# Decoder block on one core: the first norm's token scale summed from the feature-major input

## The chip, the cores and the metric

The kernel runs on one core of one Trainium2 chip. The metric is the device time of one execution in microseconds (us); less is better. A core has five engines with instruction streams of their own: PE (TensorE, matrix products; its weight loads are shown as PEld), DVE (VectorE), ACT (ScalarE), POOL (GpSimd) and SP (SyncE, which here only issues transfers). Engines wait for each other through semaphores, and each engine takes its instructions strictly in order.

## What is computed

One decoder block on 512 tokens of width 1024: a gated feed-forward (width 2816), a mixer, and a second feed-forward, each with a norm before and after it. The change concerns the start of the first feed-forward:

```
def rms_norm(x, g):
    xf = x.astype(jnp.float32)
    y = xf * lax.rsqrt(jnp.mean(xf * xf, axis=-1, keepdims=True) + NORM_EPS)
    return (y * g.astype(jnp.float32)).astype(x.dtype)

def swiglu(x, w_gu, w_down):
    g, u = jnp.split(x @ w_gu, 2, axis=-1)
    return (jax.nn.silu(g) * u) @ w_down
...
    f = swiglu(rms_norm(h, ffn1_pre_g[l]), ffn1_w_gu[l], ffn1_w_down[l])
    h = h + MACARON_SCALE * rms_norm(f, ffn1_post_g[l])
```

The norm's scale, one over the root of the mean square, is one number for each token. It can therefore be multiplied into the product with `w_gu` afterwards, as long as it is there before the gate's nonlinearity.

## The kernel before

Activations lie feature-major in the first feed-forward: features on the 128 partitions (eight chunks of 128, index `k`), the 512 tokens along the free axis. Every fp32 product is made of three matmuls on parts: a value is split into a rounded high part and the rest (a copy on ACT, a subtraction on DVE), and high times high, high times low and low times high are added up in PSUM.

Stages of the first feed-forward, in the order in which PE runs them:

1. `first_unscaled`: four output chunks (`f1f` banks) accumulate over `k = 0..7`, twelve 128x512 matmuls for each `k`, from `xk` (a 128x512 piece of `xt`, the feature-major input, in the tiles `xs`) times the norm's gain, and from `wk` (tiles `wf`). ACT makes `u1h` and the high weights, DVE makes `u1l` and the low weights. The scale is not yet applied. This loop lies in a block in which the written order holds (`tc.manual_schedule()`); elsewhere a scheduler sets each engine's order by a simulated timeline.
2. The `f1g` chunks: eight more output chunks of 24 matmuls 128x512 each, with weights that `wload` fetches (`wraw`) and `wsplit` splits into high and low (tiles `w`: line 104 on ACT, line 105 on DVE).
3. The `f1X`, `f1Y`, `f1Q` products of `paired`: the other columns in a scheme of seven block products of 128x256 matmuls, on sums of weight blocks (`f1L`, `f1R`, `f1M`, `f1N`, splits `f1W`) and of activation blocks (`u1m`).

`token_scale` makes the scale. It has the input a second time, token-major, as `xin` (four loads of 128x1024, tiles `x`): ACT squares each with a sum along the row, DVE adds the epsilon, POOL raises to the power -1/2, DVE puts the 128 values on a diagonal (`n1d`), which is split (`n1dd`) and multiplied by a matrix of ones. The product, bank `rb`, holds each token's scale on every partition, and ACT copies it to `rbc`. Its `yield 2` places these matmuls two chunks later on PE. Only then come `tail`, which multiplies the banks by `rbc` (`f1gs`, `f1us`), takes the tanh on ACT (`f1s`) and forms the gated product `f1p`, and `scaled`, which multiplies `xs` in place by gain and `rbc` (line 707) and forms the `u1m` splits.

Pools that matter: `big` (19 buffers), `t4p` (8 buffers of 128x1024: `wraw`, `x`, `f1L`, `f1R`, `u1ts`), `t2p` (10 buffers of 128x512) and eight PSUM banks. All these loads are issued by SP in one queue.

Of the kernel before, what the change touches and what calls it, by code (L numbers as in the profile page):

```python
# [8 lines left out]
F32 = mybir.dt.float32  # L9
F32R = mybir.dt.float32r  # L10
AF = mybir.ActivationFunctionType
ALU = mybir.AluOpType
# [4 lines left out]
P = 128  # L17
# [11 lines left out]
NT = T // P  # L29
D = 1024  # L30
KD = D // P
FF = 2816
KF = FF // P
EPS = 1e-6
# [8 lines left out]
def hybrid_block_kernel(ctx, tc, x, xt, g1, w_first, gains, gu1, gs1, dn1, ds1, w_x, w_gate, w_q, w_k, w_v, w_gl, w_ga, w_pl, w_pa,  # L43
                        w_o, gu2, gs2, dn2, ds2, vecs, bd, sinks, rope, mask, out):
    nc = tc.nc
    V, A, G, PE, SP = nc.vector, nc.scalar, nc.gpsimd, nc.tensor, nc.sync

    const = ctx.enter_context(tc.tile_pool(name="const", bufs=1))
# [7 lines left out]
    def bank(name):  # L56
        return psum.tile([P, 512], F32, name=name, tag="bank")

    def t4(name, dtype=F32):
        return t4p.tile([P, 1024], dtype, name=name, tag="t4")  # L60

    def t2(name, dtype=F32):
        return t2p.tile([P, 512], dtype, name=name, tag="t2")

    def b8(name, shape, dtype=F32):
        return big.tile(shape, dtype, name=name, tag="b8")

    def sm(name, n=1):
        return small.tile([P, n], F32, name=name, tag=f"sm{n}")
# [15 lines left out]
    RAHEAD = 3  # L85
# [7 lines left out]
    def wload(upto):  # L93
        while len(raws) < min(upto, wcap[0]):
            n = len(raws)
            raw = t4(f"wraw{n}")
            wdma.append(SP.dma_start(raw, worder[n]))
            raws.append(raw)

    def wsplit(upto):  # L100
        while len(wready) < min(upto, wcap[0]):
            n = len(wready)
            w = b8(f"w{n}", [P, 2, 1024], F32R)
            A.copy(w[:, 0, :], raws[n])  # L104
            V.tensor_tensor(out=w[:, 1, :], in0=raws[n], in1=w[:, 0, :].bitcast(F32),  # L105
                            op=ALU.subtract)
            wready.append((w[:, 0, :], w[:, 1, :]))
            wload(n + 1 + RAHEAD)
# [9 lines left out]
    def start(gen):  # L118
        n = next(gen, None)
        if n is not None:  # L120
            live.append([gen, n])
# [22 lines left out]
    xv = x.rearrange("(t p) d -> t p d", p=P)  # L144
# [7 lines left out]
    for k in range(KD):  # L152
        xk, wk = xs[k // 4][:, k % 4, :], wf[k // 4][:, k % 4, :]
        SP.dma_start(xk, xt[k])
        SP.dma_start(wk, w_first[k])
        first_in.append((xk, wk))
    xin = []
    for t in range(NT):
        wload(min(t + 1, RAHEAD))
        xin.append(t4(f"x_{t}"))  # L160
        SP.dma_start(xin[t], xv[t])
    ident = const.tile([P, P], F32, name="ident")
    make_identity(nc, ident)
    ones = t2("ones", F32R)[:, :P]
    G.memset(ones.bitcast(F32), 1.0)
    mhalf = const.tile([P, 1], F32, name="mhalf")
    G.memset(mhalf, -0.5)

    def rstd(ms, name):
        r = sm(name)  # L170
        G.tensor_tensor(out=r, in0=ms, in1=mhalf, op=ALU.pow)
        return r
# [4 lines left out]
    def at(u, part, k, tok):  # L177
        return u[part][k // 4][:, k % 4, tok]
# [466 lines left out]
    def moving(raw, name, mv):  # L645
        lo_, hi_ = slice(0, 256), slice(256, 512)
        t = [t4(f"{name}ts{i}").rearrange("p (k t) -> p k t", k=4) for i in range(2)]
        a, b = raw

        def split(i, z, sign=1.0):  # L650
            o = b8(f"{name}m{i}", [P, 2, 4, 256], F32R)
            mv[i] = o[:, 0], o[:, 1]
            A.activation(o[:, 0], z, AF.Copy, scale=sign)
            V.scalar_tensor_tensor(out=o[:, 1], in0=z, scalar=sign, in1=o[:, 0].bitcast(F32), op0=ALU.mult,
                                   op1=ALU.subtract)

        V.tensor_tensor(out=t[0], in0=a[:, :, lo_], in1=a[:, :, hi_], op=ALU.subtract)
        V.tensor_tensor(out=t[1], in0=b[:, :, hi_], in1=t[0], op=ALU.add)
        split(6, t[1], -1.0)
        split(5, t[0])  # L660
        yield 1
        V.tensor_tensor(out=t[0], in0=b[:, :, hi_], in1=a[:, :, hi_], op=ALU.subtract)
        split(7, t[0])
        yield 1
        V.tensor_tensor(out=t[1], in0=t[1], in1=b[:, :, lo_], op=ALU.subtract)
        split(4, t[1])
# [8 lines left out]

    rbc = t2("rbc")

    def token_scale(after):
        dhs = []
        for t in range(NT):  # L680
            ms = sm(f"n1ms{t}")
            A.activation(xin[t], xin[t], AF.Square, scale=1.0 / 32.0, accum_out=ms)
            me = sm(f"n1me{t}")
            V.tensor_scalar_add(me, ms, EPS)
            r = rstd(me, f"n1r{t}")
            d = t2(f"n1d{t}")[:, :P]
            V.tensor_scalar_mul(d, ident, r)
            dh = t2(f"n1dd{t}", F32R)[:, :2 * P].rearrange("p (s t) -> p s t", s=2)
            A.copy(dh[:, 0, :], d)
            V.tensor_tensor(out=dh[:, 1, :], in0=d, in1=dh[:, 0, :].bitcast(F32), op=ALU.subtract)  # L690
            dhs.append(dh)
        yield 2
        b = bank("rb")
        for t, dh in enumerate(dhs):
            for i in range(2):
                PE.matmul(b[:, t * P:(t + 1) * P], lhsT=ones, rhs=dh[:, i, :], start=i == 0, stop=i == 1)
        A.copy(rbc, b)
        after()
        start(scaled())

    mv1 = {}

    def scaled():
        lo_, hi_ = slice(0, 256), slice(256, 512)
        for k in range(KD):
            xk = first_in[k][0]
            V.scalar_tensor_tensor(out=xk, in0=xk, scalar=g1v[:, k:k + 1], in1=rbc, op0=ALU.mult, op1=ALU.mult)
            if k % 4 == 3:
                yield 1
        for i, half, tok in ((1, 0, lo_), (2, 1, lo_), (3, 1, hi_)):  # L710
            o, z = b8(f"u1m{i}", [P, 2, 4, 256], F32R), xs[half][:, :, tok]
            mv1[i] = o[:, 0], o[:, 1]
            A.copy(o[:, 0], z)
            V.tensor_tensor(out=o[:, 1], in0=z, in1=o[:, 0].bitcast(F32), op=ALU.subtract)
            if i == 2:
                yield 1
        yield from moving(xs, "u1", mv1)

    def first_unscaled(u, name, done):
        bs = [bank(f"{name}{i}") for i in range(4)]  # L720
        with tc.manual_schedule():
            for k in range(KD):
                xk, wk = first_in[k]
                if k % 2 == 0:
                    w = b8(f"{name}w{k}", [P, 2, 2, 512], F32R)
                wh, wl = w[:, k % 2, 0, :], w[:, k % 2, 1, :]
                uh, ul = at(u, 0, k, ALL), at(u, 1, k, ALL)
                A.activation(uh, xk, AF.Copy, scale=g1v[:, k:k + 1])
                A.copy(wh, wk)
                V.scalar_tensor_tensor(out=ul, in0=xk, scalar=g1v[:, k:k + 1], in1=uh.bitcast(F32),  # L730
                                       op0=ALU.mult, op1=ALU.subtract)
                V.tensor_tensor(out=wl, in0=wk, in1=wh.bitcast(F32), op=ALU.subtract)
                for lw, rx, n in ((wh, uh, 0), (wh, ul, 1), (wl, uh, 2)):
                    for i in range(4):
                        PE.matmul(bs[i], lhsT=lw[:, i * P:(i + 1) * P], rhs=rx, start=k == 0 and n == 0,
                                  stop=k == KD - 1 and n == 2)
        wsplit(2)
        start(token_scale(lambda: [done(i, b) for i, b in enumerate(bs)]))

    chunk1, blocked1 = gate_up(u1, "f1", first_unscaled, lambda: (gs1, mv1), lambda: rbc, ds1)  # L740
    g_post, g_pre = gain_pair(1, 2, "g_b1")
    u2 = new_u("u2")
# [17 lines left out]
    z = const.tile([P, KD], F32, name="z")  # L760
# [18 lines left out]
    for i in range(2):  # L779
        raw = t4(f"bdraw{i}")  # L780
        A.dma_start(raw, bd[i])
        t = b8(f"bd{i}", [P, 2, D], F32R)
# [193 lines left out]
    def sig_gate(c, src, name):  # L976
        w = wget()
        b = bank(f"{name}g{c}")
        feat_chunk(b, w, u2, ALL)
        s = t2(f"{name}s{c}")  # L980
        A.activation(s, b, AF.Tanh, scale=0.5)
        tick()
        wh, wl = wget()
        b = bank(f"{name}p{c}")
        for k in range(KD):
            ks = slice(k * P, (k + 1) * P)
            sh, sl = src[k // 4]
            mm3(b, wh[:, ks], wl[:, ks], sh[:, k % 4, :], sl[:, k % 4, :], k == 0, k == KD - 1)
        tick()
        return s, b  # L990
# [36 lines left out]
    for c in range(KD):  # L1027
        s, b = sig_gate(c, yl, "gl")
# [14 lines left out]
    for c in range(KD):  # L1043
        s, b = sig_gate(c, ya, "ga")
# [115 lines left out]
```

## Time and profile before

| | |
|---|---|
| time, median of 3 runs | 1137.34 us (1137.04 to 1137.84) |
| time of the profiled execution | 1137.61 us |
| span of the profiled execution | 1135.8 us, granted clock 0.998 |
| busy in the span | PE 1111.3 us (98%), DVE 889.9 (78%), ACT 579.2 (51%), POOL 72.0 (6%) |
| DMA | 147.00 MB moved; first fortieth of the span at 367 GB/s |

The time of an execution is its span and a little around it: here 1.8 us more. In the timeline a row has a start, a duration, the engine, the line, the operation with output and inputs, and in brackets how long the engine had sat idle and what released it. Instructions of one engine overlap a little, so the pace of a run of them (start to start) is shorter than the duration of one. A row of the table by stretches has the stretch, its length, then for PE, PEld, DVE, ACT and POOL the busy time and the number of instructions, the granted PE clock (1.00 is full), the busy share of the DMA engines and GB/s.

### The profile page before, as it was taken

The numbers are of one execution on the slowest core, as the hardware profiler recorded it, in microseconds if no ns is written. First come the engines' busy times: TensorE is split into PE (matmuls) and PEld (weight loads), VectorE is DVE, ScalarE is ACT, GpSimd is POOL, SyncE is SP. The second block draws the span as 40 slices with busy tenths as digits, with TensorE's granted clock in tenths as the row PEclk, the third lists the DMA queues.
The fourth block names the chain that finished last, engine by engine and source line by source line (L and its number), as shares of the span: only waits on it lengthen the run. The fifth ranks groups of instructions, "written<-read, shape, count | busy, mean of one in ns | idle before, by whom it ended". The sixth has DMA issues, their size and how long they took to land.

```text
span 1135.8 us, 16614 instructions
## 1 busy us (share of the span) xinstructions
PE 1111.3 (98%) x6584; PEld 987.5 (87%) x6584; DVE 889.9 (78%) x1250; ACT 579.2 (51%) x960; POOL 72.0 (6%) x74
## 2 busy tenths in 40 slices
PE   7999999999999999999999999999999999999997
PEld 6779999998788988887888888887999999998786
DVE  6499889978987797999777561556858889879966
ACT  7144555554744668566555341335435455455652
POOL 1000000002001011113122000000000000001000
PEclk9999999999999999999999999999999999999999
DMA  9123333258464462712822441533213333256631
GB/s 367 41 75 112 112 112 97 94 182 208 110 244 152 145 169 91 205 56 65 247 83 79 140 149 37 188 109 132 92 58 94 109 111 112 78 185 175 158 130 74
DMA packets 42909, 147.00 MB, mean 129 GB/s; under 512 B 5200, under 2 KB 5328, under 8 KB 42192
## 3 DMA queue, kind: packets, MB, share of 16 engines
q1 hardware_dynamic: 35920, 122.35, 33.4%
q0 software_dynamic: 2304, 8.39, 3.9%
q10 hardware_dynamic: 4608, 15.21, 3.7%
q8 instruction: 51, 0.84, 0.3%
q14 instruction: 26, 0.21, 0.1%
HBM read 134.39 MB, written 11.53 MB: 128 GB/s over the span
## 4 chain that ended last, share of the span: by engine, by line
PE 54%; DVE 9%; issue 2%; DMA 1%; ACT 1%; POOL 0%; DVEq 0%; POOLq 0%; ACTq 0%
PE f2X L135 4%; PE f2X L136 3%; PE f2X L134 3%; PE f2Q L136 1%; PE f2Q L135 1%; PE f2Q L134 1%; PE glg L134 1%; PE glp L134 1%; PE glp L136 1%; PE glg L136 1%; PE glg L135 1%; PE glp L135 1%; PE gap L135 1%; PE gag L135 1%; PE gag L136 1%
## 5 line engine op out<-in xcount | busy, mean ns | idle before, releaser
L105 DVE TENSOR_TENSOR w<-wraw,w 128x1024 fp32r<-128x1024 f32 x96 | 117.0, 1253 | 17.3 <-ACT w L104 15.9
L104 ACT CAST w<-wraw 128x1024 fp32r<-128x1024 f32 x96 | 96.6, 1049 | 24.5 <-PE glp L136 7.3
L136 PE MATMUL f1X<-u1m,f1W 128*128 128x256 f32 x256 | 72.5, 283 | 0.7 <-DVE f1W L344 0.7
L134 PE MATMUL f1X<-u1m,f1W 128*128 128x256 f32 x256 | 72.5, 283 | 0.2 <-ACT f1sn L364 0.2
L135 PE MATMUL f1X<-u1m,f1W 128*128 128x256 f32 x256 | 72.4, 283 | 0.0
L136 PEld LDWEIGHTS f1X<-u1m,f1W 128*128 128x128 f32 x256 | 49.1, 192 | 0.9 <-DVE f1W L344 0.9
L134 PEld LDWEIGHTS f1X<-u1m,f1W 128*128 128x128 f32 x256 | 49.1, 192 | 0.5 <-ACT f1sn L364 0.4
L135 PEld LDWEIGHTS f1X<-u1m,f1W 128*128 128x128 f32 x256 | 49.1, 192 | 0.1
L136 PE MATMUL f2X<-u3h,f2W 128*128 128x256 f32 x144 | 40.8, 283 | 0.0
L136 PE MATMUL f2X<-u3m,f2W 128*128 128x256 f32 x144 | 40.8, 283 | 0.0
L134 PE MATMUL f2Q<-u3m,f2W 128*128 128x256 f32 x144 | 40.8, 283 | 0.0
L135 PE MATMUL f2Q<-u3m,f2W 128*128 128x256 f32 x144 | 40.8, 283 | 0.0
L136 PE MATMUL f2Q<-u3m,f2W 128*128 128x256 f32 x144 | 40.8, 283 | 0.0
L135 PE MATMUL f2X<-u3l,f2W 128*128 128x256 f32 x144 | 40.8, 283 | 0.0
L135 PE MATMUL f2X<-u3m,f2W 128*128 128x256 f32 x144 | 40.8, 283 | 0.0
L134 PE MATMUL f2X<-u3m,f2W 128*128 128x256 f32 x144 | 40.7, 283 | 0.0
L134 PE MATMUL f2X<-u3h,f2W 128*128 128x256 f32 x144 | 40.7, 283 | 0.0
L534 DVE TENSOR_TENSOR f2w<-f2b,f2w 128x1024 fp32r<-128x1024 f32 x28 | 33.9, 1219 | 5.0 <-ACT f2w L533 5.0
L534 DVE TENSOR_TENSOR f1w<-f1b,f1w 128x1024 fp32r<-128x1024 f32 x28 | 33.9, 1220 | 4.8 <-ACT f1w L533 4.8
L134 PE MATMUL f1Q<-u1m,f1W 128*128 128x256 f32 x128 | 36.2, 283 | 0.0
L135 PE MATMUL f1Q<-u1m,f1W 128*128 128x256 f32 x128 | 36.2, 283 | 0.0
L136 PE MATMUL f1Q<-u1m,f1W 128*128 128x256 f32 x128 | 36.2, 283 | 0.0
(846 smaller groups left out, 3884.9 us busy)
## 6 DMA issues: line engine op xcount, KB each, us to landing
f2L<-in_gs_dram SPq DMA_DIRECT2D x18, 512.0 KB, 3.6
f2R<-in_gs_dram SPq DMA_DIRECT2D x18, 512.0 KB, 4.3
wraw<-in_gu_dram SPq DMA_DIRECT2D x16, 512.0 KB, 5.5
f1L<-in_gs_dram SPq DMA_DIRECT2D x16, 512.0 KB, 3.6
f1R<-in_gs_dram SPq DMA_DIRECT2D x16, 512.0 KB, 4.5
f1b<-in_ds_dram SPq DMA_DIRECT2D x16, 512.0 KB, 4.4
f2b<-in_ds_dram SPq DMA_DIRECT2D x16, 512.0 KB, 4.4
wraw<-in_dn_dram SPq DMA_DIRECT2D x12, 512.0 KB, 7.3
```

The source lines that it names most:

```text
L104: A.copy(w[:, 0, :], raws[n])
L105: V.tensor_tensor(out=w[:, 1, :], in0=raws[n], in1=w[:, 0, :].bitcast(F32), op=ALU.subtract)
L134: PE.matmul(o, lhsT=ah, rhs=bh, start=start, stop=False, skip_group_check=reopen)
L135: PE.matmul(o, lhsT=ah, rhs=bl, start=False, stop=False, skip_group_check=reopen)
L136: PE.matmul(o, lhsT=al, rhs=bh, start=False, stop=stop, skip_group_check=reopen)
L534: V.tensor_tensor(out=w[:, 1], in0=z, in1=w[:, 0].bitcast(F32), op=ALU.subtract)
```

## The change

The token-major input is no longer loaded at the start. In the loop over `k` ACT also squares `xk` (times 1/32 before squaring, so that the sum over all features is the mean square), and DVE adds the squares up in one accumulator `acc` (tile `f1fsq`). In the last turn of the loop the accumulator is split into two parts, `n1h` and `n1l`, and PE multiplies both by the matrix of ones: the sum over the partitions then stands in every partition of the bank `rb`. ACT takes the root with the epsilon as bias, DVE the reciprocal, in `rbc`. Four weight chunks are split ahead of this instead of two, and `scaled` yields after each of its three splits.

```diff
-    xin = []
-    for t in range(NT):
-        wload(min(t + 1, RAHEAD))
-        xin.append(t4(f"x_{t}"))
-        SP.dma_start(xin[t], xv[t])
+    wload(RAHEAD)
...
+    eps = const.tile([P, 1], F32, name="eps")
+    G.memset(eps, EPS)
...
-    def token_scale(after):
...
-            A.activation(xin[t], xin[t], AF.Square, scale=1.0 / 32.0, accum_out=ms)
...
-            r = rstd(me, f"n1r{t}")
...
-        yield 2
...
-                PE.matmul(b[:, t * P:(t + 1) * P], lhsT=ones, rhs=dh[:, i, :], start=i == 0, stop=i == 1)
-        A.copy(rbc, b)
-        after()
-        start(scaled())
...
-            if i == 2:
-                yield 1
+            yield 1
...
+    rb = bank("rb")
+
+    def token_sums(acc):
+        ah = t2("n1h", F32R)
+        al = t2("n1l", F32R)
+        A.copy(ah, acc)
+        V.tensor_tensor(out=al, in0=acc, in1=ah.bitcast(F32), op=ALU.subtract)
+        for i, z in enumerate((ah, al)):
+            PE.matmul(rb, lhsT=ones, rhs=z, start=i == 0, stop=i == 1)
...
+        acc = t2(f"{name}sq0")
...
+                sq = acc if k == 0 else t2(f"{name}sq{k}")
+                A.activation(sq, xk, AF.Square, scale=1.0 / 32.0)
...
+                if k > 0:
+                    V.tensor_tensor(out=acc, in0=acc, in1=sq, op=ALU.add)
+                if k == KD - 1:
+                    token_sums(acc)
...
-        wsplit(2)
-        start(token_scale(lambda: [done(i, b) for i, b in enumerate(bs)]))
+            wsplit(4)
+            A.activation(rbc, rb, AF.Sqrt, bias=eps)
+            V.reciprocal(rbc, rbc)
+            for i, z in enumerate(bs):
+                done(i, z)
+        start(scaled())
```

The instruction streams of both kernels are the same from the `f1X` stage on, line numbers, buffer numbers and the place of the last `f1s` steps aside. What differs before it stands in three places. The first is SP's queue behind the sixteen loads of `xs` and `wf` (piece of the difference; `wraw` are raw weights):

```order
 L97 DMA wraw_97<-in_gu_dram 128x1024
-L161 DMA x_99<-in_x_dram 128x1024
+L97 DMA wraw_99<-in_gu_dram 128x1024
 L97 DMA wraw_101<-in_gu_dram 128x1024
-L161 DMA x_103<-in_x_dram 128x1024
-L97 DMA wraw_105<-in_gu_dram 128x1024
-L161 DMA x_107<-in_x_dram 128x1024
-L161 DMA x_109<-in_x_dram 128x1024
```

The four loads of `x` are gone, and the raw weights follow each other.

The second is DVE between the last low weights of `first_unscaled` and the low part of the fifth `f1g` weight chunk. Before (from the fourth weight split on, `w_348`; `w_418` is the fifth chunk's):

```order
L105 TENSOR_TENSOR w_348<-wraw_267,w_348 128x1024
L690 TENSOR_TENSOR n1dd_315<-n1d_313,n1dd_315 128x128
L280 TENSOR_TENSOR f1gs_389<-f1f_125,rbc 128x512
L281 TENSOR_TENSOR f1us_390<-f1f_126,rbc 128x512
L707 SCALAR_TENSOR_TENSOR xs_77<-xs_77,g1v,rbc 128x512 x4
L707 SCALAR_TENSOR_TENSOR xs_78<-xs_78,g1v,rbc 128x512 x4
...
L280 TENSOR_TENSOR f1gs_487<-f1g_423,rbc 128x512
...
L281 TENSOR_TENSOR f1us_488<-f1g_455,rbc 128x512
L105 TENSOR_TENSOR w_418<-wraw_272,w_418 128x1024
L105 TENSOR_TENSOR w_452<-wraw_321,w_452 128x1024
```

After (`w_302` is the fourth split, `w_397` the fifth chunk's):

```order
L721 TENSOR_TENSOR f1fsq_124<-f1fsq_124,f1fsq_264 128x512
L699 TENSOR_TENSOR n1l<-f1fsq_124,n1h 128x512
L105 TENSOR_TENSOR w_287<-wraw_97,w_287 128x1024
...
L105 TENSOR_TENSOR w_302<-wraw_290,w_302 128x1024
L730 RECIPROCAL rbc<-rbc 128x512
L278 TENSOR_TENSOR f1gs_310<-f1f_120,rbc 128x512
L279 TENSOR_TENSOR f1us_311<-f1f_121,rbc 128x512
L682 SCALAR_TENSOR_TENSOR xs_77<-xs_77,g1v,rbc 128x512 x4
L682 SCALAR_TENSOR_TENSOR xs_78<-xs_78,g1v,rbc 128x512 x4
...
L278 TENSOR_TENSOR f1gs_462<-f1g_402,rbc 128x512
L689 TENSOR_TENSOR u1m_386<-xs_77,u1m_386 128x1024
L105 TENSOR_TENSOR w_397<-wraw_295,w_397 128x1024
```

The norm's small steps are gone from between the splits, the reciprocal stands where DVE waited for `rbc`, and the fifth split no longer stands behind the fourth chunk's `f1us` step but behind a `u1m` step.

The third is PE, where the ones product moved from behind the second `f1g` chunk to the last turn of `first_unscaled`, ahead of that turn's own twelve matmuls. After:

```order
L726 MATMUL f1f_123<-u1h_115,f1fw_242 128x512
L701 MATMUL rb<-n1h,ones 128x512
L701 MATMUL rb<-n1l,ones 128x512
L726 MATMUL f1f_120<-u1h_115,f1fw_242 128x512
L726 MATMUL f1f_121<-u1h_115,f1fw_242 128x512
```

Before, it was these eight small matmuls behind the second `f1g` chunk:

```order
L136 MATMUL f1g_353<-u1h_121,w_269 128x512
L696 MATMUL rb<-n1dd_282,ones 128x128 x2
L696 MATMUL rb<-n1dd_293,ones 128x128 x2
L696 MATMUL rb<-n1dd_304,ones 128x128 x2
L696 MATMUL rb<-n1dd_315,ones 128x128 x2
L134 MATMUL f1g_423<-u1h_120,w_318 128x512
```

On ACT two table loads are new, ahead of the root (`L729`) and ahead of the next tanh (`L281`).

More of the change, by code (lines that the diff above doesn't have):

```diff
@@ L676, in hybrid_block_kernel @@
     rbc = t2("rbc")
-    def token_scale(after):
-        dhs = []
-        for t in range(NT):
-            ms = sm(f"n1ms{t}")
-            A.activation(xin[t], xin[t], AF.Square, scale=1.0 / 32.0, accum_out=ms)
-            me = sm(f"n1me{t}")
-            V.tensor_scalar_add(me, ms, EPS)
-            r = rstd(me, f"n1r{t}")
[L686 to L691, printed above, removed]
-        yield 2
[L693 to L697, printed above, removed]
-        after()
-        start(scaled())
     mv1 = {}
```

## The prediction

> **What bounds the kernel now.** I read the page's busy shares first, then the waits of PE, longest in total first, then a table by stretches around the one place where they gather. In a row of waits stand who waited, for whom, the sum in us, how often, and the longest.
>
> ```profile
> span 1135.8 us, 16614 instructions
> PE 1111.3 (98%) x6584; PEld 987.5 (87%) x6584; DVE 889.9 (78%) x1250; ACT 579.2 (51%) x960; POOL 72.0 (6%) x74
> ...
> PE f1f L735 <- ACT f1fw L729: 6.2, 1, 6.2
> PE f1g L134 <- ACT w L104: 3.8, 3, 2.1
> ...
> PE f1X L136 <- DVE f1W L344: 0.7, 1, 0.7
> ...
> 30.28:41.16 10.88, 10.88 (x49) 9.01 (x48) 0.00 (x0) 0.00 (x0) 0.00 (x0) 1.00 0.09 38
> 41.16:42.29 1.13, 1.13 (x10) 1.08 (x9) 0.00 (x0) 0.09 (x1) 0.00 (x0) 1.00 0.00 0
> 42.29:53.00 10.71, 10.71 (x48) 8.63 (x46) 10.18 (x16) 1.77 (x3) 0.00 (x0) 1.00 0.00 0
> 53.00:58.45 5.45, 1.62 (x6) 0.60 (x5) 5.45 (x9) 5.41 (x7) 0.00 (x0) 1.00 0.00 0
> 58.45:62.13 3.68, 3.68 (x8) 2.50 (x9) 3.68 (x4) 3.68 (x5) 0.00 (x0) 0.54 0.38 132
> 62.13:81.22 19.09, 19.09 (x85) 15.77 (x84) 19.09 (x23) 4.80 (x7) 0.00 (x0) 1.00 0.27 85
> 81.22:84.09 2.87, 2.87 (x25) 2.82 (x23) 2.87 (x6) 1.99 (x3) 0.00 (x0) 1.00 0.01 3
> 84.09:86.88 2.79, 1.95 (x14) 1.59 (x13) 2.79 (x4) 1.23 (x3) 0.00 (x0) 1.00 0.19 28
> ```
>
> PE is the bound: it is idle for only 24.5 us of the span, 6.2 of them at the start. The largest later wait, `f1g` for the high weights, lies in the first feed-forward, just where the change works. PE's pace there: 48 matmuls of 128x512 in 10.88 us are 0.227 each, and 24 of 128x256 in 2.87 are 0.12. From 30.28, the first `f1g` matmul, to 86.88, the first of `f1Q`, PE has 192 of the former and 36 of the latter: 43.5 + 4.3 = 47.8 us. It took 56.6, so 8.8 are lost: 0.9 to the ones product and the restart behind it; 4.5 in 53.00 to 58.45 (5.45 less four matmuls); 1.6 in the next stretch, where the granted clock is 0.54 (3.68 less nine); 1.4 at the end, where twelve small matmuls took 2.79 and not 1.44; and 0.4 scattered. The rows behind the wait:
>
> ```profile
> 41.16 1.00 PE L696 MATMUL rb<-n1dd,ones 128*128 128x128 f32 x8
> ...
> 42.20 0.59 ACT L697 COPY rbc<-rb 128x512 f32<-128x512 f32 x1 [16.36 <-PE rb L696]
> ...
> 42.82 0.69 DVE L280 TENSOR_TENSOR f1gs<-f1f,rbc 128x512 f32<-128x512 f32 x1 [15.96 <-ACT rbc L697]
> 44.03 5.38 DVE L707 SCALAR_TENSOR_TENSOR xs<-xs,g1v,rbc 128x512 f32<-128x512 f32 x8
> 49.33 0.69 DVE L280 TENSOR_TENSOR f1gs<-f1f,rbc 128x512 f32<-128x512 f32 x1
> 49.93 0.69 DVE L281 TENSOR_TENSOR f1us<-f1f,rbc 128x512 f32<-128x512 f32 x1
> ...
> 53.04 0.63 ACT L283 ACTIVATE f1s<-f1gs 128x512 f32<-128x512 f32 x1 [2.36 <-DVE f1gs L280]
> 53.58 1.98 ACT L104 CAST w<-wraw 128x1024 fp32r<-128x1024 f32 x2
> ...
> 54.66 0.50 PE L134 MATMUL f1g<-u1h,w 128*128 128x512 f32 x1 [1.50 <-ACT w L104]
> 58.45 0.66 PE L134 MATMUL f1g<-u1h,w 128*128 128x512 f32 x1 [2.10 <-ACT w L104]
> ...
> 58.20 2.35 DVE L105 TENSOR_TENSOR w<-wraw,w 128x1024 fp32r<-128x1024 f32 x2
> ```
>
> The chain reads backwards. PE stood for the fifth chunk's weights; ACT cast them at 53.58, because three `f1s` steps stand ahead in its queue, and they waited for DVE; DVE subtracted them at 58.20, because 15 us of scale work came first, and that waited for `rbc`, which came at 42.8 because the ones product stands behind two `f1g` chunks on PE. DVE sat idle for 16 us, and the backlog then hit PE.
>
> **The change part by part.** Prices for the new work:
>
> ```profile
> 5.70 0.75 DVE L730 SCALAR_TENSOR_TENSOR u1l<-xs,g1v,u1h 128x512 fp32r<-128x512 f32 x1 [5.70 <-ACT u1h L728]
> ...
> 8.24 0.74 DVE L730 SCALAR_TENSOR_TENSOR u1l<-xs,g1v,u1h 128x512 fp32r<-128x512 f32 x1
> 9.50 0.75 DVE L730 SCALAR_TENSOR_TENSOR u1l<-xs,g1v,u1h 128x512 fp32r<-128x512 f32 x1
> ...
> 7.22 0.72 ACT L728 ACTIVATE u1h<-xs,g1v 128x512 fp32r<-128x512 f32 x1
> 8.35 0.72 ACT L728 ACTIVATE u1h<-xs,g1v 128x512 fp32r<-128x512 f32 x1
> ...
> L213 ACT ACTIVATE b1qsq<-b1qz 128x512 f32<-128x512 f32 x8 | 5.1, 632 | 8.6 <-DMA b1rh<-in_x_dram 5.1 <-DVE b1qz L212 3.1 <-DVE b1nme L184 0.4
> ...
> 9.35 0.33 SPq L97 DMA_DIRECT2D wraw<-in_gu_dram  x1
> 10.03 0.33 SPq L161 DMA_DIRECT2D x<-in_x_dram  x1
> ...
> wraw<-in_gu_dram SPq DMA_DIRECT2D x16, 512.0 KB, 5.5
> ...
> 407.31 1.28 ACT L815 ACT_TABLE_LOAD   x1
> 408.61 1.92 ACT L815 ACTIVATE lm<-lm 128x2048 f32<-128x2048 f32 x1
> ...
> L765 DVE RECIPROCAL q<-q x1: 196/196/196, 326.2 to 326.2; 128x8 f32<-128x8 f32 x1
> ...
> L932 DVE RECIPROCAL at11ss<-at11ss x1: 163/163/163, 513.3 to 513.3; 128x4 f32<-128x4 f32 x1
> ...
> L932 DVE RECIPROCAL at33ss<-at33ss x1: 181/181/181, 638.3 to 638.3; 128x4 f32<-128x4 f32 x1
> ```
>
> Squares and sums in the loop: ACT goes from 1.13 us for each `k` (7.22 to 8.35) to at most 1.76 with a Square at 0.63; DVE from 1.26 (8.24 to 9.50) to 1.86 with an add at the 0.60 pace. DVE ends the loop at 5.70 + 1.26 + 7 x 1.86 = 20.0, and `n1h` and `n1l` add 0.6 and 0.7: 21.3. PE takes 12 x 0.227 = 2.72 for each `k`, so it enters the last turn at 30.28 - 2.72 = 27.56. What hides this work is PE's own length in the loop, with 6 us to spare; cost nothing, at most a microsecond if the first turns trip.
>
> Ones product: two matmuls of 128x512, 0.45 us on PE instead of 0.9; all that follows starts at 30.73.
>
> Removed: four loads, four squares, the diagonals and POOL's powers. On DVE and ACT they lay in front of the 16 us idle time, so they return nothing. SP loses four issues; the raw weights move ahead. SP issues one each 0.68 (9.35 to 10.03), so the fourth, needed by ACT at about 24, leaves near 11.4 and lands 5.5 later. `f1L` and `f1R` now wait for the third and fourth splits, near 26, and are first read by DVE near 68: hidden. The `eps` fill is hidden by the start.
>
> Scale: the second ones matmul ends near 28.2. The table load sits behind the wait for `rb`, so 1.28 counts, then the root at 0.6 (the copy's 0.59): 30.1. The next table load, for tanh, runs beside DVE's eight `xs` steps. For a reciprocal of 128x512 no row exists. The sixteen 128x4 rows lie between the two quoted, so from 4 to 8 elements it grew by 15 to 33 ns, 3.8 to 8.3 ns each: 2.1 to 4.4 us for 512. The floor is any 128x512 step, 0.69. I take 3.0, near the middle of the growth, since the 128x8 row lies above all the 128x4 ones. `rbc` is there at 33.1 instead of 42.8.
>
> The Trainium skill, "ScalarE: Activation LUTs", section "What ACT_TABLE_LOAD costs", gives a drain of 1.38 us beside the load, 2.66 for a switch. The row here differs: the ACTIVATE starts 0.02 after its load ends. By the page the scale would come 1.4 later.
>
> DVE from 33.1: two steps at the 0.60 pace (49.33 to 49.93), the eight `xs` steps in 5.3 (44.03 to 49.33), then up to the third chunk's `f1gs` eleven more at 0.60 and two of 128x1024, and `u1m` and the split, four at 1.18 (half of 2.35) in all. That is 1.2 + 5.3 + 6.6 + 4.7 = 17.8: `w_397` is whole at 50.9. PE asks for its low part after four chunks and four matmuls: 30.73 + 21.8 + 0.9 = 53.4. ACT has the high part near 47.5, as its third `f1s` waits for DVE until 45. So 2.5 us are to spare, the wait is gone, and with it the half clock, which follows the idle time. The next three splits come every 2.3 us, and PE takes one in 5.4.
>
> What is late next: `f1W` of the first sums. Its subtraction stands behind the last chunk's `f1us`, which needs PE's last `f1g` matmul at 74.26 (30.73 + 43.5). DVE then does `f1us`, two sums and the split: 74.5 + 1.8 + 1.2 = 77.5. PE asks at 74.26 + 2.87 + 0.24 = 77.4. The wait of 1.4 shrinks to about 0.3, not to nothing; if ACT's copies are late, up to 1.4 stay.
>
> Sum: of 8.8 lost, 0.45 + 0.3 remain; gain 8.0. Behind the `f1X` stage the streams stand in the same order and PE bounds them, so the shift carries to the end. The profiled execution took 1137.61, which gives 1129.6; the median of the runs is 0.3 lower: 1129.3.
>
> **Rivals.** First, *the scale is still late*. If the reciprocal passes 3.0 + 2.5 = 5.5 us, PE waits at the fifth chunk for the excess, and over 2 us of waiting brings back the half clock with its 1.6. For it: no row of this size. Against it: the growth between the two small sizes. By rows the worst growth gives 4.4 us: no wait. With part of the `f1X` wait kept, up to 1132. The Trainium skill, "VectorE: DVE Perf Modes", section "First, the fixed hardware budget", says that the reciprocal iterates its divide eight times; read as eight passes of 0.60 that would be an estimate of 4.8 us, with the drain above `w_397` comes at 54, and the time would be 1130. The rows show a slope between one pass and eight.
>
> Second, *slower*: the ones product stands ahead of the last twelve matmuls in PE's queue, so everything behind it waits for `n1l`. PE meets it at 27.56, and it is expected at 21.3. Each microsecond beyond 27.56 costs one; the gain of 8.0 is gone at 35.6. That would need adds of 2.6 us each, over four times the row's 0.60, or squares that stall on a table load in each turn: eight pairs of 1.28 are 20 us, `n1l` at 41, and 1129.3 + 13.4 + 1.6 for the half clock is 1144. Against it: the order shows one table load at the start and none in the loop.
>
> Third, *the gain is given back*: if DVE, not PE, sets the pace in the products that follow, the saved time returns as waits there, 1136 to 1138. For it: DVE is busy without a gap from 42.8 to 86.88. Against it: that was the backlog, and PE's waits behind it are a few tenths.
>
> **How the numbers follow.** The forecast, 1128.2 to 1131, has 0.78; the late scale, 1131 to 1135, 0.13; slower by the queue 0.04; given back 0.05. The range is 1128.2 to 1132.5: the lower end takes nothing lost at `f1X` (0.3) and the spread of the runs shown (0.8); the upper end takes in the `f1X` wait kept whole (1.1), a microsecond in the loop, and a first part of the late scale. A change of 0.2% (2.3 us) is about what a measurement of this kernel can tell from none. Faster by more than that: 0.78 + 0.13 = 0.91; the same, given back, 0.05; slower 0.04.
>
> **What would show it.** `rb` near 28 and `f1gs` of `f1f` near 33 in the timeline; no `f1g` wait for `w` in PE's waits; granted clock 1.00 from 50 to 70; the first `f1X` matmul near 74.3; a short `f1X` wait for `f1W`. A wait of PE at `rb`, or a reciprocal over 5.5 us, would make it wrong.

## The result, and the profile after

| | before | after |
|---|---|---|
| time, median of 4 runs each | 1137.59 us (1137.04 to 1138.47) | 1128.63 us (1128.07 to 1129.37) |
| ratio | | 0.9921, 95% interval 0.9904 to 0.9938 |
| profiled execution, its span | 1137.61 us, 1135.8 | 1128.07 us, 1126.3 |

The changed kernel is 9.0 us faster; 8.0 were forecast, and 1129.3 us. A later series ran the changed kernel five more times, with a median of 1130.86 us (1128.55 to 1131.34) against 1137.24 us of before: ratio 0.9938, interval 0.9925 to 0.9950, a gain of 6.4. Over both series the median of the nine runs of after is 1129.24 us, that of the thirteen of before 1137.34 us: 8.1, a figure that hangs on how many runs each series had. The last section shows where the 2.8 us between the two profiled executions of the changed kernel come from.

The page after begins with the busy shares. PE's busy time fell by 4.4 us and the span by 9.5. So about half of the gain is idle time that is gone. Most of the other half is the smaller ones product and matmuls that no longer run slowly or restart; some of it is a start of PE that was shorter in this execution:

```profile
span 1126.3 us, 16594 instructions
PE 1106.9 (98%) x6578; PEld 985.9 (88%) x6578; DVE 895.1 (79%) x1247; ACT 580.2 (52%) x959; POOL 69.4 (6%) x71
```

PE's waits after, longest first (who waits, for whom, sum, how often, longest). Before, `f1g <- ACT w` with 3.8 us stood second and `f1X L136 <- DVE f1W` with 0.7 was in the list. Neither is now:

```profile
PE f1f L726 <- ACT f1fw L714: 6.1, 1, 6.1
PE f2f L134 <- ACT u3h L196: 1.5, 1, 1.5
PE at02t L934 <- POOL at02s L928: 1.2, 1, 1.2
PE f1X L135 <- DVE f1w L532: 0.7, 2, 0.4
```

The table by stretches after, over the same 30.28 to 86.88, then over the `f1g` stage and over the stage from the first `f1X` to the first `f1Q` matmul (length; busy time and instructions of PE, PEld, DVE, ACT, POOL; granted clock, DMA share, GB/s):

```profile
30.28:86.88 56.60, 56.59 (x302) 48.95 (x301) 55.46 (x71) 25.73 (x33) 0.00 (x0) 1.00 0.19 57
29.86:73.38 43.52, 43.52 (x193) 36.04 (x192) 42.69 (x52) 16.74 (x19) 0.00 (x0) 1.00 0.17 52
73.38:77.96 4.58, 4.57 (x38) 4.37 (x36) 4.38 (x6) 2.94 (x5) 0.00 (x0) 1.00 0.11 11
```

Before, the row from the first `f1g` matmul to the first of `f1Q` was:

```profile
30.28:86.88 56.60, 51.94 (x237) 42.01 (x236) 44.06 (x57) 18.96 (x23) 0.00 (x0) 0.97 0.15 46
```

PE was idle there for 4.66 us and busy for 51.94. After, its two stages take 43.52 and 4.58 us, together 48.10, and PE is busy in 48.09 of them, at a granted clock of 1.00. The `f1g` stage lasts 43.52 us, which is its 192 matmuls at 0.227 and nothing more. The second stage lasts 4.58, for 36 matmuls of 0.12, which are 4.32. The rows behind it, from the timeline:

```profile
21.10 0.69 DVE L699 TENSOR_TENSOR n1l<-f1fsq,n1h 128x512 fp32r<-128x512 f32 x1 [0.69 <-ACT n1h L698]
26.69 0.39 PE L701 MATMUL rb<-n1h,ones 128*128 128x512 f32 x1
26.91 0.39 PE L701 MATMUL rb<-n1l,ones 128*128 128x512 f32 x1
27.14 1.07 PE L726 MATMUL f1f<-u1h,f1fw 128*128 128x512 f32 x4
27.41 1.28 ACT L729 ACT_TABLE_LOAD   x1 [2.52 <-PE rb L701]
28.70 0.69 ACT L729 ACTIVATE rbc<-rb,eps 128x512 f32<-128x512 f32 x1
29.42 3.35 DVE L730 RECIPROCAL rbc<-rbc 128x512 f32<-128x512 f32 x1 [2.74 <-ACT rbc L729]
29.86 0.39 PE L134 MATMUL f1g<-u1h,w 128*128 128x512 f32 x1
32.88 0.69 DVE L278 TENSOR_TENSOR f1gs<-f1f,rbc 128x512 f32<-128x512 f32 x1
49.39 1.22 DVE L105 TENSOR_TENSOR w<-wraw,w 128x1024 fp32r<-128x1024 f32 x1
73.38 0.28 PE L134 MATMUL f1X<-u1m,f1W 128*128 128x256 f32 x1
76.37 0.28 PE L135 MATMUL f1X<-u1m,f1W 128*128 128x256 f32 x1
76.66 0.39 PE L136 MATMUL f1X<-u1m,f1W 128*128 128x256 f32 x1
77.96 0.28 PE L134 MATMUL f1Q<-u1m,f1W 128*128 128x256 f32 x1
```

The first multiplication by the scale (`f1gs`) starts at 32.88; before it was 42.82. The fifth chunk's low weights (the `w` row) are whole at 50.61. PE asks for them 100 matmuls after 29.86, at 52.5: 1.9 us to spare.

### The profile page after: what moved, and what is told of

Same layout as the page of the kernel before. It is cut to its first block, busy times and chain, and to the rows that moved or that the text cites. A ratio compares the mean times of both kernels' runs of the same rounds, so it can differ in the third digit from the quotient of the medians.

```text
span 1126.3 us, 16594 instructions
## 1 busy us (share of the span) xinstructions
PE 1106.9 (98%) x6578; PEld 985.9 (88%) x6578; DVE 895.1 (79%) x1247; ACT 580.2 (52%) x959; POOL 69.4 (6%) x71
## 4 chain that ended last, share of the span: by engine, by line
PE 79%; DVE 12%; issue 3%; DMA 2%; ACT 2%; POOL 0%; DVEq 0%; POOLq 0%; ACTq 0%
PE f2X L135 4%; PE f2X L136 4%; PE f2X L134 3%; PE f1X L136 3%; PE f1X L135 3%; PE f1X L134 3%; PE f1f L726 2%; PE f2Q L136 1%; PE f2Q L135 1%; PE f2Q L134 1%; PE f1Q L136 1%; PE f1Q L135 1%; PE f1Q L134 1%; DVE f1w L532 1%; PE glg L134 1%
## 5 line engine op out<-in xcount | busy, mean ns | idle before, releaser
L136 PE MATMUL f1X<-u1m,f1W 128*128 128x256 f32 x256 | 72.6, 283 | 0.0
L136 PEld LDWEIGHTS f1X<-u1m,f1W 128*128 128x128 f32 x256 | 49.1, 192 | 0.2 <-DVE f1W L342 0.2
L136 PE MATMUL f2X<-u3h,f2W 128*128 128x256 f32 x144 | 40.8, 283 | 0.0
L136 PE MATMUL f2X<-u3m,f2W 128*128 128x256 f32 x144 | 40.8, 283 | 0.0
L136 PE MATMUL f2Q<-u3m,f2W 128*128 128x256 f32 x144 | 40.8, 283 | 0.0
L136 PE MATMUL f1Q<-u1m,f1W 128*128 128x256 f32 x128 | 36.2, 283 | 0.0
```

The source lines that it names most:

```text
L136: PE.matmul(o, lhsT=al, rhs=bh, start=False, stop=stop, skip_group_check=reopen)
```

## The experiments

Two theories were set against each other. *S*: the gain is the moment at which DVE gets the scale, together with four weight chunks split ahead, which keep PE fed until DVE is through; what the scale is computed from does not matter. *X*: the gain is the work that went, the four loads with their places in SP's queue, or the lighter steps. A third, *D*, came up on the way: DVE is so close to being the bound that every microsecond of it costs one.

One number carries them all, the length from the first `f1g` matmul to the first `f1Q`. PE alone needs 47.8 us for it. The medians come from several series, and the start of PE varies between executions; the length leaves the start out. From the timelines of all runs:

| kernel | first `f1g` | first `f1Q` | length | median of the runs, us |
|---|---|---|---|---|
| before | 30.28 | 86.88 | 56.60 | 1137.34 |
| after | 29.86 | 77.96 | 48.10 | 1128.63 |
| after, second series | 31.37 | 79.47 | 48.10 | 1130.86 |
| 1 before, scale at once, four splits | 31.20 | 79.27 | 48.07 | 1130.18 |
| 2 after, scale two chunks later | 30.30 | 92.07 | 61.77 | 1142.28 |
| 3 after, with the loads of `x` | 31.03 | 79.12 | 48.09 | 1128.66 |
| 4 after, two splits | 31.00 | 87.32 | 56.32 | 1137.39 |
| 5 after, one further reciprocal | 31.05 | 82.35 | 51.30 | 1132.81 |
| 6 after, two further reciprocals | 30.74 | 85.51 | 54.77 | 1135.67 |
| 7 after, half a further reciprocal | 30.95 | 79.65 | 48.70 | 1129.93 |
| 8 after, no reciprocal | 30.12 | 77.95 | 47.83 | 1129.54 |

### 1. The old scale, without its wait

The kernel before keeps its token-major input, its four loads, diagonals and all. Only the ones product no longer waits two chunks, and four chunks are split ahead:

```diff
-        yield 2
+        if T == 0:
+            yield 2
...
-        wsplit(2)
+            wsplit(4)
```

> The kernel before, with its token-major input and its own scale, but with four weight chunks split ahead and the ones product put directly behind the first loop instead of two f1g chunks later. Theory S (only the moment counts at which DVE gets the scale, with four splits ready): rbc near 32, fifth low weights whole near 49.6, PE asks at 53.4, so no f1g wait and no half clock; 8.8 lost less 0.9 for the eight small ones matmuls and 0.3 at f1X leave a gain of 7.6, 1130 us. Rival X (the four loads not made are what helps, they hold up the queue and the buffers): 1136 to 1138. Rival K (the lighter steps on DVE and POOL help): 1134 to 1137.

Measured: 1130.18 us (1129.48 to 1130.80), ratio 0.9935, interval 0.9922 to 0.9949. From its timeline, the ones product and the first `f1gs`:

```profile
30.48 0.89 PE L697 MATMUL rb<-n1dd,ones 128*128 128x128 f32 x7
31.96 0.23 PE L697 MATMUL rb<-n1dd,ones 128*128 128x128 f32 x1
32.84 0.69 DVE L280 TENSOR_TENSOR f1gs<-f1f,rbc 128x512 f32<-128x512 f32 x1 [5.50 <-ACT rbc L698]
```

The scale reaches DVE at 32.84, where the changed kernel has 32.88, and the length is 48.07. Two edits that touch neither the input, nor the arithmetic, nor the yields in `scaled` give the whole stage gain. That is theory S. The 1.5 us to the first series of after are no larger than the 2.2 between the two series of after. In the profiled executions the first `f1g` comes 1.34 later than in after: 1.0 of that is a slower start of PE (the last section), and 0.3 the price of the old ones product, which takes 0.72 us ahead of that matmul (30.48 to 31.20) where the new one takes 0.45.

### 2. The new scale, late again

The sums in the loop stay. Ones product, root and reciprocal come two chunks later, as `yield 2` had it:

```diff
+    def late(bs, done):
+        yield 2
+        for i, z in enumerate(halves):
+            PE.matmul(rb, lhsT=ones, rhs=z, start=i == 0, stop=i == 1)
+        A.activation(rbc, rb, AF.Sqrt, bias=eps)
+        V.reciprocal(rbc, rbc)
...
-        start(scaled())
+        start(late(bs, done))
```

> The changed kernel with its sums from the feature-major input and without the token-major loads, but the ones product, root, reciprocal and all that uses them two f1g chunks later, as before. S: the ones product ends near 40.7, table load 1.3, root 0.7 and reciprocal 3.35 put f1gs near 46.2, 3.4 later than in the kernel before, so its whole loss is back and about 3 more: 1139 to 1142 us, with the half clock. X and K: the loads and small steps are still gone, so most of the gain stays, 1128 to 1131.

Measured: 1142.28 us (1141.89 to 1143.35), ratio 1.0043, interval 1.0030 to 1.0057, just above the 1139 to 1142 that theory S expected. PE's waits and the timeline of DVE:

```profile
PE f1g L134 <- ACT w L104: 7.1, 2, 6.5
PE f1g L136 <- DVE w L105: 0.8, 1, 0.8
...
43.92 3.35 DVE L709 RECIPROCAL rbc<-rbc 128x512 f32<-128x512 f32 x1 [17.16 <-ACT rbc L708]
47.38 0.69 DVE L278 TENSOR_TENSOR f1gs<-f1f,rbc 128x512 f32<-128x512 f32 x1
```

With the same new arithmetic and no token-major loads the kernel is slower than before, since `f1gs` comes at 47.38, 4.6 later than the 42.82 of before. DVE sits idle for 17 us first, and PE pays afterwards for the same weights. The arithmetic without its early place is a loss.

### 3. The loads put back

The changed kernel, with the four loads of `x` at their old places in SP's queue, read by nobody:

```diff
-    wload(RAHEAD)
+    xin = []
+    for t in range(NT):
+        wload(min(t + 1, RAHEAD))
+        xin.append(t4(f"x_{t}"))
+        SP.dma_start(xin[t], xv[t])
```

> The changed kernel, but the four token-major loads of 512 KB are issued again at their old places in the queue, and nobody reads them. S: 1128.6 within 0.5 us, since the weights still land ahead of their splits. X: 2 MB at 0.37 MB per us are 5.6 us of transfers, so 1131 to 1134.

Measured: 1128.66 us (1128.07 to 1130.07), ratio 0.9921, interval 0.9908 to 0.9935: the same as after, and a length of 48.09. The 2.1 MB that are no longer moved are worth nothing here, which ends the first part of theory X. Its second part, the lighter steps, fell with experiments 1 and 2: the old steps have the whole stage gain, and the new ones by themselves have none.

### 4. Two splits ahead instead of four

```diff
-            wsplit(4)
+            wsplit(2)
```

> The changed kernel with two weight chunks split ahead of the scale instead of four. S: the third chunk's split stands behind 16 us of scale work on DVE that starts at 32.9, whole near 48.9, while PE asks near 41.2: about 7.7 us of waiting and 1.6 of half clock, so 1137 to 1139, the gain gone. A theory by which the early scale alone is enough: 1128 to 1131.

Measured: 1137.39 us (1135.77 to 1138.18), ratio 0.9995, interval 0.9986 to 1.0004. The whole gain is gone, though the first `f1gs` starts at 34.03. PE's timeline and waits:

```profile
PE f1g L134 <- ACT w L104: 5.5, 1, 5.5
...
47.54 0.80 PE L134 MATMUL f1g<-u1h,w 128*128 128x512 f32 x1 [5.49 <-ACT w L104]
```

PE runs out of weights at the third chunk, while DVE and ACT do the scale's work. An early scale starts 17.7 us of DVE work (32.88 to 50.61 in after), and PE has to be fed for that long. At 5.4 us a chunk, two chunks don't last and four do. In the kernel before, DVE had split four chunks ahead of the scale too (the fourth at 25.44), but PE had used up two of them when the scale came at 42.82. The old, late scale with `wsplit(4)` was not run.

### 5 to 8. How much the reciprocal may cost

The reciprocal was the price with no row. It was repeated into a buffer that nothing reads (one, two, half a time), and once left out. Where it is left out the root itself is used as the scale, so the division isn't computed. In each of these the scheduler also changes the order of a few steps. Ahead of the fifth split they balance: from the first `f1gs` to that split DVE takes 16.5 us in after (32.88 to 49.39) and with one or half a further reciprocal alike (37.27 to 53.72, 35.57 to 52.02).

```diff
             V.reciprocal(rbc, rbc)
+            for i in range(1):
+                V.reciprocal(t2(f"spare{i}"), rbc)
```

> The changed kernel with one further reciprocal of 128x512 on DVE, into a spare tile, between the scale and its first use: 3.4 us more delay. In the changed kernel the fifth low weights are whole at 50.6 and PE asks at 52.1 to 52.5, so 1.5 to 1.9 us are to spare. S: PE waits 1.5 to 1.9 there, short enough to keep the clock: 1130.1 to 1130.8 us, up to 1132.4 if the half clock comes. A theory by which DVE is the bound in the whole stage: all of the 3.4, 1132. One by which the scale's moment is covered anyway: 1128.6.

Measured: 1132.81 us (1132.33 to 1135.18), ratio 0.9967, interval 0.9955 to 0.9980. That is 4.2 over the first series of after, more than either theory expected (1130.1 to 1132.4, and 1132). PE's waits in its profiled execution:

```profile
PE f1X L134 <- ACT f1sn L362: 0.9, 1, 0.9
...
PE f1g L136 <- DVE w L105: 0.7, 1, 0.7
PE f1X L136 <- DVE f1W L342: 0.7, 1, 0.7
```

The expected wait at the fifth chunk is there. The `f1g` stage lasts 44.92 (31.05 to the first `f1X` at 75.97) for 43.52: of the 3.35 us, 1.40 are lost there, and 1.95 fitted into the slack. The rest, 1.8 of the 3.2 by which the length grew, is two waits at `f1X` that weren't expected: DVE hadn't caught up, and the scheduler had put the sums for `f1W` further back. The median grew by more than the length because PE also started later here (31.05 for 29.86). So the expectation of theory S missed, and for a while theory D stood: 3.2 us for 3.35 of DVE.

> The same with two further reciprocals, 6.8 us of delay; one f1us step also comes ahead of the split. S: fifth low weights near 58, PE waits some 4 to 5.5 and the half clock's 1.6 comes back: 1134 to 1136 us. DVE as the bound: 1135.4. Covered: 1128.6.

Measured: 1135.67 us (1134.48 to 1137.86), ratio 0.9990, interval 0.9980 to 0.9999. PE's waits, and the timeline at the first of them:

```profile
PE f1g L134 <- ACT w L104: 3.1, 2, 1.9
PE f1g L136 <- DVE w L105: 0.8, 1, 0.8
...
54.56 0.50 PE L134 MATMUL f1g<-u1h,w 128*128 128x512 f32 x1 [1.90 <-ACT w L104]
56.46 0.80 PE L134 MATMUL f1g<-u1h,w 128*128 128x512 f32 x1 [1.16 <-ACT w L104]
58.49 0.79 PE L136 MATMUL f1g<-u1h,w 128*128 128x512 f32 x1 [0.81 <-DVE w L105]
...
55.00:60.00 5.00, 3.03 (x8) 1.73 (x7) 5.00 (x6) 5.00 (x6) 0.00 (x0) 0.54 0.11 13
```

With 6.6 us more on DVE nearly the whole picture of before is back: three waits close together, and, from the second of them on, a granted clock of 0.54 and eight matmuls in 5 us. The 1135.67 lie in what theory S expected and next to the 1135.4 of theory D. The waits add up to 3.9, but the length grew by 6.7. As in before, the slow clock makes up much of what the list of waits doesn't show.

One and two reciprocals lengthen the stage by 3.2 and 6.7 us for the 3.35 and 6.6 that they add, which is what theory D says. The half and the missing one decide:

```diff
             V.reciprocal(rbc, rbc)
+            V.reciprocal(t2("spare")[:, :256], rbc[:, :256])
```

> The changed kernel with one further reciprocal of 128x256 (half the size) behind the first, into a buffer that nothing reads; the scheduler also puts one more f1gs step and its tanh ahead of the fifth split. Theory S (the slack counts: the fifth low weights have 1.5 to 2.4 us to spare): DVE is 1.7 later at w and 0.6 for the further f1gs step, so w is whole near 52.9 to 54 and PE, which asks at 52.1 to 53.3, waits 0 to 0.9 there; a few tenths more in the f1X stage; 1128.6 to 1130.2. Rival D (DVE is the pace, each us of DVE ahead of the splits costs one): the full reciprocal cost 4.2 for 3.35 and two cost 7.0 for 6.7, so half of one costs 1.7 to 2.1: 1130.3 to 1130.7.

```diff
-            V.reciprocal(rbc, rbc)
```

> The changed kernel without the reciprocal: the root itself is used as the scale, so this leaves out the division and its 3.35 us of DVE. Theory S (PE waits for nothing that DVE could bring earlier): no gain beyond the 0.2 of the f1X wait, 1128.2 to 1128.8. Rival D (DVE is the pace): 1.5 to 3 us faster, 1125.5 to 1127.

Measured with the half: 1129.93 us (1128.97 to 1130.61), ratio 0.9932, interval 0.9919 to 0.9946. Without a reciprocal: 1129.54 us (1127.85 to 1129.80), ratio 0.9927, interval 0.9914 to 0.9939. The changed kernel itself in that series, same chip, had 1130.86 and 0.9938. The three intervals overlap, and 1129.54 lies above what either theory expected without a reciprocal (1128.2 to 1128.8, and 1125.5 to 1127), so the times don't decide. The profiles do. DVE with the half, the ends of its two stages and PE's only longer wait in them; then the two ends of the `f1g` stage without a reciprocal:

```profile
33.90 1.75 DVE L731 RECIPROCAL spare<-rbc 128x256 f32<-128x256 f32 x1
52.02 1.21 DVE L105 TENSOR_TENSOR w<-wraw,w 128x1024 fp32r<-128x1024 f32 x1
...
30.95 0.39 PE L134 MATMUL f1g<-u1h,w 128*128 128x512 f32 x1
74.47 0.28 PE L134 MATMUL f1X<-u1m,f1W 128*128 128x256 f32 x1
78.35 0.39 PE L136 MATMUL f1X<-u1m,f1W 128*128 128x256 f32 x1 [0.62 <-DVE f1W L342]
```

```profile
30.12 0.39 PE L134 MATMUL f1g<-u1h,w 128*128 128x512 f32 x1
73.64 0.28 PE L134 MATMUL f1X<-u1m,f1W 128*128 128x256 f32 x1
```

Both `f1g` stages last 43.52 us, exactly as in after. With the half reciprocal the fifth low weights are whole at 53.23 and PE asks near 53.6, so 0.4 us is left of the slack, and the `f1X` stage is 0.6 longer. Without the reciprocal that stage is 0.27 shorter, and that is all that 3.35 us less of DVE bring. So DVE is not the pace: theory D falls, and the slack that the prediction counted on is real: 1.9 us (50.61 to 52.5 in after), and 1.95 by experiment 5. Past it, further DVE time costs PE about as much again: in experiment 5 by the wait at the fifth chunk and the late `f1W`, in experiment 6 by longer waits and the slow clock.

### The changed kernel once more

> The changed kernel once more, unaltered, for its spread and for a second profile of its start. If the 0.8 us by which its first profile was shorter ahead of the first f1g matmul (29.86 with the ones product in it) belong to the change, f1g starts again near 29.9 and the time is 1128.6. If they belong to that one execution, f1g starts between 30.7 and 31.1 as in the four variants profiled since, f1Q near 79, and the profiled execution takes 1129 to 1130; the median stays at 1128.6 within 0.5.

Measured: 1130.86 us (1128.55 to 1131.34). Of the two expectations the second was the nearer one, and it missed too: `f1g` started at 31.37, later still than 31.1, `f1Q` at 79.47, the profiled execution took 1130.86, and the median wasn't within 0.5 of 1128.6. So the 0.8 us of the first profile belong to that execution, not to the change. The last section reads it.

## Why the prediction held, point by point

- *The loop hides the squares and sums.* `n1l` starts at 21.10 and is done at 21.8, for 21.3 worked out; PE comes to it at 26.69. Nothing was lost, and the rival of a late `n1l` did not come.
- *The ones product costs 0.45.* 26.69 to 27.14 is 0.45.
- *The scale at 33.1.* It was 32.88. The reciprocal was mis-sized: 3.35 us, for 3.0 taken and 2.1 to 4.4 as bounds. The root took 0.69 instead of 0.6. That 32.88 is so near is luck: the table load started 0.8 earlier than forecast (27.41 for 28.2), since the loop's slow beginning was shorter in this execution, and that made up for both. In the second series the first `f1gs` came at 34.4, with PE equally later.
- *The table load counts, the drain doesn't.* The root starts at 28.70, 0.01 after its load has ended. The drain of 1.38 us that the Trainium skill, "ScalarE: Activation LUTs", section "What ACT_TABLE_LOAD costs", adds to the load isn't in this trace. Nor are the 4.8 us for the reciprocal, an estimate from eight passes by the Trainium skill, "VectorE: DVE Perf Modes", section "First, the fixed hardware budget": the measured 3.35 lies below it.
- *17.8 us of DVE, fifth weights at 50.9, 2.5 to spare.* 17.7, 50.61 and 1.9. The spare time was forecast too large by 0.6 since PE, too, ran ahead of the forecast, by 0.9: 52.5 for 53.4. Experiments 5 and 7 put the real edge between 1.75 and 3.35 us of further DVE work, where a slack of 1.9 must have it, and the 1.40 lost in experiment 5 put it at 1.95.
- *With the wait the half clock goes.* The granted clock is 1.00 over the whole stretch. Experiment 6 shows the reverse, waits and 0.54 together. That over 2 us of waiting bring the half clock, as the first rival had it, no run shows as an edge: it followed waits of 1.5 and 0.4 us in two of eleven profiles and not in the other nine (the last section).
- *The `f1X` wait shrinks from 1.4 to 0.3.* Of 5.66 us of before for this stage 4.58 are left, 0.26 above its 4.32; of these, 0.17 is the gap at 76.66 (76.37 and 0.12 make 76.49). The prediction's own times (77.4 and 77.5) give a wait of 0.1; it took 0.3 without a row for the difference.
- *The gain carries to the end.* From the first `f1Q` on the profiled executions took 1050.7 us before (1137.61 - 86.88) and 1050.1 after. Where the length is that of after it was 1050.2 to 1051.4 (experiments 1 and 3, and the second series). Nothing that the experiments can tell was given back.

The sum was 8.0. In the stretch it is 56.60 - 48.10 = 8.50, less 0.45 for the ones product, which now lies ahead of the first `f1g`: 8.05. The two profiled executions differ by 9.54: these 8.05, then 0.87 from PE's shorter start (29.86 less 0.45, for 30.28), and 0.62 from behind the first `f1Q`. The forecast had no term for either, and in the second profile of after the start went the other way. So the length confirms the sum; how near the medians come to it (9.0, 6.4, and 8.1 over both series) is partly luck. No step of the forecast failed. Its weak place was the reciprocal, where any price up to about 5 us gave nearly the same time.

## What to carry to other kernels

Where a value is needed only after a product, look at how long the engine that will use it stands idle before it comes, and at what stands behind that work in its queue: here 16 us of an idle DVE came back as 8 us of PE two chunks later, in a wait that names only the weights. Bringing the value forward helps only if the fed engine has stock for as long as the burst of work that follows, so the place in the order and the number of chunks split ahead had to change together. A cost that lies in slack has an edge, not a slope: to see whether an engine is the bound, take work away from it as well as adding some.

## What the runs showed of the hardware

*A reciprocal on DVE.* 128x512 took 3.35 us and 128x256 1.75, 6.3 ns for each further element. A subtraction of 128x512 took 0.69. The slope between 4 and 8 elements (3.8 to 8.3 ns) had been a fair guide.

*The start of PE has no fixed length.* PE's first rows in the changed kernel, first and second series (the first `f1f` matmuls, in groups as the timeline joins them):

```profile
6.13 2.07 PE L726 MATMUL f1f<-u1h,f1fw 128*128 128x512 f32 x4 [6.13 <-ACT f1fw L714]
8.01 1.58 PE L726 MATMUL f1f<-u1l,f1fw 128*128 128x512 f32 x4
9.42 2.01 PE L726 MATMUL f1f<-u1h,f1fw 128*128 128x512 f32 x8
11.27 1.07 PE L726 MATMUL f1f<-u1l,f1fw 128*128 128x512 f32 x4
```

```profile
6.35 2.07 PE L726 MATMUL f1f<-u1h,f1fw 128*128 128x512 f32 x4 [6.35 <-ACT f1fw L714]
8.22 1.91 PE L726 MATMUL f1f<-u1l,f1fw 128*128 128x512 f32 x4
9.93 3.02 PE L726 MATMUL f1f<-u1h,f1fw 128*128 128x512 f32 x8
12.78 1.07 PE L726 MATMUL f1f<-u1l,f1fw 128*128 128x512 f32 x4
```

Start to start, the first kernel's groups of 4, 4 and 8 take 1.88, 1.41 and 1.85 us; full pace (0.227 each) would be 0.91, 0.91 and 1.82. So the slow phase ends within the second group. In the second series they take 1.87, 1.71 and 2.85, and it ends only in the third. A slow matmul takes 0.43 (1.71 by four), so the phase lasts about 2.9 us in the one and 5.8 in the other. Over the sixteen matmuls that is 1.3 us, and with 0.2 of a later start it is the 1.5 by which the first `f1g` comes later (29.86 and 31.37); the profiled executions differ by 2.8. No wait stands in PE's rows in this phase. The table's granted clock says 1.00 for 8 to 14 us in both, so this phase is seen only in the pace of the matmuls. The Trainium skill, "TensorE: Matmul & The Clock Gate", section "What's actually happening", says that the clock is released by a window of activity that runs freely and doesn't start with the kernel, so that one kernel shows a different number of slow matmuls from run to run; it gives the window as 3.4 us. The rows agree that the length varies, here by more than the 0.5 us to either side that this section of the Trainium skill gives; that no edit made the difference follows from the two profiles being of one kernel.

*The same waits, and the half clock only sometimes.* The other 1.3 us lie far behind. From the first `f1Q` matmul to the first `f2f` matmul, the start of the second feed-forward's first product (780.02 and 781.57), both profiles took the same, 702.06 and 702.10 us. There PE waits twice in both, 1.5 us and then 0.4. PE from 784 to 787 us, first and second series:

```profile
784.00:787.00 3.00, 3.00 (x27) 3.00 (x27) 1.59 (x4) 2.57 (x4) 0.55 (x1) 1.00 0.83 329
```

```profile
784.00:787.00 3.00, 3.00 (x16) 3.00 (x16) 2.39 (x3) 2.31 (x6) 0.00 (x0) 0.51 0.94 354
```

Behind the same waits the clock is full in the one and half in the other, with sixteen matmuls instead of 27, and from the first `f2f` to the end the second execution is 1.24 us longer. 1.51, 0.04 and 1.24 are the whole 2.79. All eleven profiles have these two waits; experiment 5 has the half clock behind them too (0.53 from 787 to 790 us), the other nine have 1.00. Why it follows in two of them the runs don't show.

Two medians of one kernel here lie 2.2 us apart (1128.63 and 1130.86), so smaller differences between two series can't be read from the times. The length of the stage can: it repeated within 0.03 us in four profiles of three kernels.
